# Batch normalisation on one core: tiles of even and odd channels, first tile split at a quarter

## The chip, the cores and the metric

The kernel runs on one core of one Trainium2 chip. The metric is the device time of one execution in microseconds (us). The input is read from the chip's external memory (DRAM) into the on-chip memory of 128 partitions, changed there, and written back; transfers are made by the core's 16 DMA engines. SyncE (SP) and ScalarE (ACT) each issue transfers on a queue of their own; VectorE (DVE) does most of the arithmetic.

## The reference

The input x has the shape 32 x 256 x 128 x 128 (images, channels, height, width) in float32, 537 MB. Each channel has four parameters. The whole computation is one multiplication and one addition for each element:

```python
return gamma * (x - mean) / np.sqrt(var + eps) + beta
```

With scale = gamma / sqrt(var + eps) and shift = beta - mean * scale it is out = x * scale + shift, with one scale and one shift for each channel.

## The kernel before

One image's 256 channels are two tiles of 128 channels: the lower half (channels 0 to 127) and the upper half (128 to 255). A partition holds one channel, 16384 values or 64 KB. So there are NT = 64 tiles of 8.39 MB, and a tile is one contiguous block of DRAM. Tile i uses column i % NCB (NCB is 2) of the scales and shifts.

There are three buffers for tiles (NBUF = 3), and the order of the work is written out by hand with semaphores. Each tile is loaded by SP, changed in place by VectorE (L122, one instruction with a scale and a shift for each partition), and stored by ScalarE's queue (L133). The load of tile i waits for the store of tile i - 3, which used the same buffer (L94 and the wait behind it). VectorE waits for the tile's load; the store waits for VectorE. Each queue takes its work in the order written.

Tile 0 is different: it is loaded in two parts, left (L84) and right (L91), the two halves of its columns, and VectorE changes them in two instructions. Its store waits for both. Between the two loads SP issues the four loads of parameters (L87): each brings 256 values to 16 partitions of the tile rows, which VectorE has set to zero before (L85). The last tile is different too: VectorE changes its first 9216 columns (VCOLS) and ScalarE the others (L145), side by side.

The parameters arrive with the channels along a row, and are needed with one channel in each partition. VectorE transposes rows in blocks of 32 x 32 (L100), and four copies put the blocks' first columns into the tile par (L105). ScalarE takes the square root (L107), and VectorE the reciprocal, the scale and the shift (L114 to L117). Every VectorE step here waits for the one before through the semaphore vec; the transpose waits for the four loads (the semaphore fetched) instead. The first tile's instructions follow these steps in VectorE's queue.

Of the kernel before, what the change touches and what calls it, by code (L numbers as in the profile page):

```python
# [1 line left out]

# [4 lines left out]


NBUF = 3

VCOLS = 9216


@with_exitstack
def kernel(
    ctx: ExitStack,
    tc: tile.TileContext,
    x: bass.AP,
    gamma: bass.AP,
    beta: bass.AP,  # L20
    running_mean: bass.AP,
    running_var: bass.AP,
    out: bass.AP,
):
    nc = tc.nc
    eps = 1e-5
    f32 = mybir.dt.float32

    N, C, H, W = x.shape
    P = nc.NUM_PARTITIONS  # L30
    assert C % P == 0
    NCB = C // P
    HW = H * W
    NT = N * NCB
    B = 32
    NQ = P // B
    NE = 16
    NPAR = 4

    xr = x.rearrange("n (cb p) h w -> (n cb) p (h w)", p=P)  # L40
    outr = out.rearrange("n (cb p) h w -> (n cb) p (h w)", p=P)

    params = ctx.enter_context(tc.tile_pool(name="params", bufs=1))
    data = ctx.enter_context(tc.tile_pool(name="data", bufs=1))
    bufs = [data.tile([P, HW], f32, name=f"t{s}", tag=f"t{s}") for s in range(NBUF)]
    rows = params.tile([B, NPAR * C], f32, name="rows", tag="rows")
    turned = params.tile([B, NPAR * C], f32, name="turned", tag="turned")
    par = params.tile([P, NPAR, NCB], f32, name="par", tag="par")
    eps_t = params.tile([P, 1], f32, name="eps_t", tag="eps")
    std_t = params.tile([P, NCB], f32, name="std_t", tag="std")  # L50
    rstd_t = params.tile([P, NCB], f32, name="rstd_t", tag="rstd")
    scale_t = params.tile([P, NCB], f32, name="scale_t", tag="scale")
    ms_t = params.tile([P, NCB], f32, name="ms_t", tag="ms")
    shift_t = params.tile([P, NCB], f32, name="shift_t", tag="shift")

    loaded = [tc.alloc_semaphore(f"loaded{s}") for s in range(NBUF)]
    stored = [tc.alloc_semaphore(f"stored{s}") for s in range(NBUF)]
    early = tc.alloc_semaphore("early")  # L60
    done = tc.alloc_semaphore("done")
    fetched = tc.alloc_semaphore("fetched")
    vec = tc.alloc_semaphore("vec")
    act = tc.alloc_semaphore("act")

    with tc.tile_critical():  # L66
        count = [0]

        def step(inst, sem=None, value=None):

            if sem is not None:
                inst._wait_ge(sem, value)
            elif count[0]:
                inst._wait_ge(vec, count[0])
            inst.then_inc(vec, 1)
            count[0] += 1
            return count[0]

        left, right = slice(0, HW // 2), slice(HW // 2, HW)
        last = NT - 1  # L80

        nc.sync.dma_start(out=bufs[0][:, left], in_=xr[0][:, left]).then_inc(early, 16)  # L84
        zeroed = step(nc.vector.memset(rows[:], 0.0))  # L85
        for r, ap in enumerate((running_var, gamma, beta, running_mean)):
            inst = nc.sync.dma_start(out=rows[0:NE, r * C : (r + 1) * C], in_=ap.partition_broadcast(NE))  # L87
            if r == 0:
                inst._wait_ge(vec, zeroed)
            inst.then_inc(fetched, 16)  # L90
        nc.sync.dma_start(out=bufs[0][:, right], in_=xr[0][:, right]).then_inc(loaded[0], 16)  # L91
        for i in range(1, NT):
            s, turn = i % NBUF, i // NBUF
            inst = nc.sync.dma_start(out=bufs[s][:], in_=xr[i]).then_inc(loaded[s], 16)  # L94
            if turn:
                inst._wait_ge(stored[s], 16 * turn)


        step(nc.vector.memset(eps_t[:], eps))  # L99
        step(nc.vector.transpose(out=turned[:], in_=rows[:]), fetched, 16 * NPAR)  # L100

        blocks = turned.rearrange("p (rc q b) -> p rc q b", q=NQ, b=B)
        flat = par.rearrange("p r cb -> p (r cb)")
        for q in range(NQ):
            placed = step(nc.vector.tensor_copy(out=flat[q * B : (q + 1) * B], in_=blocks[:, :, q, 0]))  # L105
        var_t, gamma_t, beta_t, mean_t = (par[:, r] for r in range(NPAR))
        nc.scalar.activation(  # L107
            out=std_t[:],
            in_=var_t,
            func=mybir.ActivationFunctionType.Sqrt,  # L110
            bias=eps_t[:],
            scale=1.0,
        )._wait_ge(vec, placed).then_inc(act, 1)
        step(nc.vector.reciprocal(out=rstd_t[:], in_=std_t[:]), act, 1)  # L114
        step(nc.vector.tensor_mul(out=scale_t[:], in0=gamma_t, in1=rstd_t[:]))  # L115
        step(nc.vector.tensor_mul(out=ms_t[:], in0=mean_t, in1=scale_t[:]))  # L116
        ready = step(nc.vector.tensor_sub(out=shift_t[:], in0=beta_t, in1=ms_t[:]))  # L117
        nc.vector.wait_ge(vec, ready)

        def compute(i, cols=slice(0, HW)):  # L120
            t, cb = bufs[i % NBUF], i % NCB
            return nc.vector.tensor_scalar(  # L122
                out=t[:, cols],
                in0=t[:, cols],
                scalar1=scale_t[:, cb : cb + 1],
                scalar2=shift_t[:, cb : cb + 1],
                op0=mybir.AluOpType.mult,
                op1=mybir.AluOpType.add,
            ).then_inc(done, 1)

        def store(i, after):
            s = i % NBUF
            nc.scalar.dma_start(out=outr[i], in_=bufs[s][:])._wait_ge(done, after).then_inc(stored[s], 16)  # L133

        compute(0, left)._wait_ge(early, 16)
        compute(0, right)._wait_ge(loaded[0], 16)
        store(0, 2)
        for i in range(1, last):
            compute(i)._wait_ge(loaded[i % NBUF], 16 * (i // NBUF + 1))
            store(i, i + 2)  # L140

        turns = last // NBUF + 1
        compute(last, slice(0, VCOLS))._wait_ge(loaded[last % NBUF], 16 * turns)
        t, cb = bufs[last % NBUF], last % NCB
        nc.scalar.activation(  # L145
            out=t[:, VCOLS:],
            in_=t[:, VCOLS:],
            func=mybir.ActivationFunctionType.Identity,
            bias=shift_t[:, cb : cb + 1],
            scale=scale_t[:, cb : cb + 1],  # L150
        )._wait_ge(loaded[last % NBUF], 16 * turns).then_inc(done, 1)
        store(last, last + 3)

        for s in range(NBUF):
            nc.sync.wait_ge(stored[s], 16 * ((NT - s + NBUF - 1) // NBUF))


# [1 line left out]
_INS = ['x', 'gamma', 'beta', 'running_mean', 'running_var']  # L159
_OUTS = [((32, 256, 128, 128), 'float32')]  # L160


# [23 lines left out]
```

## Time and profile before

| | |
|---|---|
| median of 4 runs | 2517.73 us |
| lowest and highest of them | 2506.21 and 2518.33 us |
| profiled execution, its own time | 2513.88 us |
| profiled execution, its span | 2512.1 us |
| VectorE busy | 564.0 us (22%) |
| ScalarE busy | 7.9 us |
| moved by the DMA engines | 1073.84 MB, mean 427 GB/s |
| one tile's VectorE instruction | 8.81 us |
| median from issue to landing, load and store | 63.3 and 45.3 us |
| first store issued | 28.1 us |
| last load landed, last store issued | 2483.2 and 2489.6 us |

The span is the time from the first to the last recorded instruction of the program; the execution's own time is 1.8 us longer. The row of DMA digits in a profile cuts the span in 40 slices and gives the mean busy share of the 16 DMA engines in tenths, with 9 for 90% or more. In a list of waits, a line gives who waited, for what, the sum in us, how often, and the longest. In a timeline a line gives the start and the duration in us, the engine, the line of the kernel, the operation with its output and inputs, and in brackets how long the engine sat idle before it and what ended that.

### The profile page before, as it was taken

To read this page: it belongs to the slowest core of one execution; us is meant where nothing else is said; L and a number is where in the kernel's file an instruction comes from. 1 tells how busy PE (TensorE), PEld (TensorE's weight loads), DVE (VectorE), ACT (ScalarE), POOL (GpSimd) and SP (SyncE) were. 2 spreads that over 40 slices of the span, in tenths; PEclk is the share of its full clock that TensorE was granted. 3 is DMA by queue.
4 is the path that set the end of the run, shared out by engine and by line. 5 is a ranking of instruction groups with operands and counts; after the bars stand their busy time and mean duration, and the time that the engine had idled before them with its cause. 6 is when DMAs were issued, how large, how long until landed. Compare 5 with 4: busy or idle time off the path is not lost.

```text
span 2512.1 us, 266 instructions
## 1 busy us (share of the span) xinstructions
DVE 564.0 (22%) x76; ACT 7.9 (0%) x3; POOL 0.2 (0%) x4
## 2 busy tenths in 40 slices
DVE  3121221212212122121221212212122122221221
ACT  0000000000000000000000000000000000000001
POOL 0000000000000000000000000000000000000000
DMA  9999999999999999999999999999999999999997
GB/s 418 433 432 434 433 434 433 433 433 434 429 434 431 432 433 430 431 432 429 432 422 433 420 424 431 432 433 429 422 434 431 426 430 432 423 428 428 429 431 332
DMA packets 18707, 1073.84 MB, mean 427 GB/s; under 512 B 2128, under 2 KB 2192, under 8 KB 2192
## 3 DMA queue, kind: packets, MB, share of 16 engines
q1 hardware_dynamic: 9488, 536.94, 49.9%
q10 hardware_dynamic: 9216, 536.88, 49.7%
q14 instruction: 3, 0.02, 0.0%
HBM read 536.94 MB, written 536.87 MB: 427 GB/s over the span
## 4 chain that ended last, share of the span: by engine, by line
another core or an unknown queue 76%; DVE 22%; DMA 1%; ACT 0%; issue 0%; SPq 0%; ACTq 0%; DVEq 0%
DVE t L122 22%; DMA t<-in_x_dram 1%; ACT t L145 0%; SPq L87 0%; DVE rows L85 0%; ACTq L133 0%; DVE eps_t L99 0%; DVEq L181 0%; SPq L66 0%
## 5 line engine op out<-in xcount | busy, mean ns | idle before, releaser
L122 DVE TENSOR_SCALAR t<-t,scale_t,shift_t 128x16384 f32<-128x16384 f32 (+2 forms) x65 | 560.6, 8624 | 1910.4 <-DMA t<-in_x_dram 1910.3
L145 ACT ACTIVATE t<-t,shift_t,scale_t 128x7168 f32<-128x7168 f32 x1 | 6.4, 6361 | 2466.7 <-DMA t<-in_x_dram 2466.7
L100 DVE STREAM_TRANSPOSE turned<-rows 32x1024 f32<-32x1024 f32 x1 | 1.2, 1232 | 11.9 <-DMA rows<-in_running_mean_dram 11.9
L107 ACT ACT_TABLE_LOAD x1 | 1.3, 1283 | 0.9 <-SPq L66 0.9
L85 DVE MEMSET rows<- 32x1024 f32 x1 | 0.9, 912 | 1.2 <-SPq L66 1.2
L105 DVE COPY par<-turned 32x8 f32<-32x8 f32 x4 | 0.6, 161 | 0.1
L107 ACT ACTIVATE std_t<-par,eps_t 128x2 f32<-128x2 f32 x1 | 0.3, 295 | 14.0 <-DVE par L105 14.0
L114 DVE RECIPROCAL rstd_t<-std_t 128x2 f32<-128x2 f32 x1 | 0.2, 166 | 0.4 <-ACT std_t L107 0.4
L116 DVE TENSOR_TENSOR ms_t<-par,scale_t 128x2 f32<-128x2 f32 x1 | 0.2, 161 | 0.0
L117 DVE TENSOR_TENSOR shift_t<-par,ms_t 128x2 f32<-128x2 f32 x1 | 0.2, 161 | 0.0
L115 DVE TENSOR_TENSOR scale_t<-par,rstd_t 128x2 f32<-128x2 f32 x1 | 0.2, 160 | 0.0
L170 POOL MEMSET const-bfloat16-1.0<- 128x1 bf16 x1 | 0.1, 102 | 0.0
L170 POOL MEMSET const-uint8-127<- 128x1 uint8 x1 | 0.1, 101 | 0.0
L170 POOL MEMSET const-float32-0.0<- 128x1 f32 x1 | 0.1, 99 | 0.2 <-issue 0.2
L170 POOL MEMSET const-float32-1.0<- 128x1 f32 x1 | 0.1, 98 | 0.0
L99 DVE MEMSET eps_t<- 128x1 f32 x1 | 0.1, 59 | 0.1
## 6 DMA issues: line engine op xcount, KB each, us to landing
t<-in_x_dram SPq DMA_DIRECT2D x2, 4096.0 KB, 16.1
out_dram<-t ACTq DMA_DIRECT2D x64, 45.3
t<-in_x_dram SPq DMA_DIRECT2D x63, 63.3
rows<-in_running_var_dram SPq DMA_DIRECT2D x1, 16.0 KB, 11.2
rows<-in_gamma_dram SPq DMA_DIRECT2D x1, 16.0 KB, 11.1
rows<-in_beta_dram SPq DMA_DIRECT2D x1, 16.0 KB, 10.9
rows<-in_running_mean_dram SPq DMA_DIRECT2D x1, 16.0 KB, 10.7
```

The costliest lines, as they stand in the source:

```text
L85: zeroed = step(nc.vector.memset(rows[:], 0.0))
L99: step(nc.vector.memset(eps_t[:], eps))
L100: step(nc.vector.transpose(out=turned[:], in_=rows[:]), fetched, 16 * NPAR)
L105: placed = step(nc.vector.tensor_copy(out=flat[q * B : (q + 1) * B], in_=blocks[:, :, q, 0]))
L107: nc.scalar.activation(out=std_t[:], in_=var_t, func=mybir.ActivationFunctionType.Sqrt, bias=eps_t[:], scale=1.0,)._wait_ge(vec, placed).t ...
L114: step(nc.vector.reciprocal(out=rstd_t[:], in_=std_t[:]), act, 1)
L115: step(nc.vector.tensor_mul(out=scale_t[:], in0=gamma_t, in1=rstd_t[:]))
L116: step(nc.vector.tensor_mul(out=ms_t[:], in0=mean_t, in1=scale_t[:]))
L117: ready = step(nc.vector.tensor_sub(out=shift_t[:], in0=beta_t, in1=ms_t[:]))
L122: return nc.vector.tensor_scalar(out=t[:, cols], in0=t[:, cols], scalar1=scale_t[:, cb : cb + 1], scalar2=shift_t[:, cb : cb + 1], op0=myb ...
L145: nc.scalar.activation(out=t[:, VCOLS:], in_=t[:, VCOLS:], func=mybir.ActivationFunctionType.Identity, bias=shift_t[:, cb : cb + 1], scale ...
L170: nc = _bacc.Bacc("TRN2", target_bir_lowering=False, num_devices=1)
```

## The change

A tile now holds every second channel of an image: tile 2n holds the even channels of image n, tile 2n + 1 the odd ones. Partition p holds channel 2p + cb instead of channel cb * 128 + p. In DRAM a tile's 64 KB rows then lie 128 KB apart, and the two tiles of an image share its 16.8 MB.

The parameters have to follow. A new tile lined takes a copy of rows in which the channels of each parameter are put in the new order (first the even, then the odd ones); the transpose then reads lined. The copy takes over the wait for the four loads, and the transpose waits for the copy.

The first tile is split at a quarter of its columns (4096 and 12288) instead of at half.

```diff
-    xr = x.rearrange("n (cb p) h w -> (n cb) p (h w)", p=P)
-    outr = out.rearrange("n (cb p) h w -> (n cb) p (h w)", p=P)
+
+    xv = x.rearrange("n (p cb) h w -> n cb p (h w)", cb=NCB)
+    outv = out.rearrange("n (p cb) h w -> n cb p (h w)", cb=NCB)
+    xr = [xv[i // NCB, i % NCB] for i in range(NT)]
+    outr = [outv[i // NCB, i % NCB] for i in range(NT)]
...
+    lined = params.tile([B, NPAR * C], f32, name="lined", tag="lined")
...
-        left, right = slice(0, HW // 2), slice(HW // 2, HW)
+        left, right = slice(0, HW // 4), slice(HW // 4, HW)
...
-        step(nc.vector.memset(eps_t[:], eps))
-        step(nc.vector.transpose(out=turned[:], in_=rows[:]), fetched, 16 * NPAR)
+        step(nc.vector.memset(eps_t[:], eps))
+        step(
+            nc.vector.tensor_copy(
+                out=lined.rearrange("b (r cb p) -> b r cb p", r=NPAR, cb=NCB),
+                in_=rows.rearrange("b (r p cb) -> b r cb p", r=NPAR, cb=NCB),
+            ),
+            fetched,
+            16 * NPAR,
+        )
+
+        step(nc.vector.transpose(out=turned[:], in_=lined[:]))
```

## The prediction

> **What bounds the kernel now.** I first read the page for what is busy, then the engines' waits, then the time order at both ends, and last the DMA share in stretches of one tile each.
>
> The page's busy shares, its DMA row and its issues come first:
>
> ```profile
> span 2512.1 us, 266 instructions
> DVE 564.0 (22%) x76; ACT 7.9 (0%) x3; POOL 0.2 (0%) x4
> DMA  9999999999999999999999999999999999999997
> DMA packets 18707, 1073.84 MB, mean 427 GB/s; under 512 B 2128, under 2 KB 2192, under 8 KB 2192
> q10 hardware_dynamic: 9216, 536.88, 49.7%
> t<-in_x_dram SPq DMA_DIRECT2D x63, 63.3
> ```
>
> The compute engines are idle for most of the time and the DMA engines never are, except in the last slice. The store queue's 9216 packets over 64 stores are 144 for each store. The 2128 packets under 512 B are 16 for each of the program's 133 transfers (64 stores, 69 loads). That leaves 128 data packets for one store, which is one for each partition: a packet is one channel's 64 KB row.
>
> The waits say that VectorE waits for loads and nothing else of weight, and that the load queue waits for stores:
>
> ```profile
> DVE t L122 <- DMA t<-in_x_dram: 1910.3, 64, 31.4
> SPq L94 <- DMA out_dram<-t: 2393.8, 61, 66.9
> ```
>
> One buffer's turn is closed: load 63.3 us, compute 8.8 us and store 45.3 us (medians from the page and from the instructions of L122) make 117.4 us, three times 39.1 us. So the step of a tile is 39 us, and in it 16.78 MB move (8.39 MB in, 8.39 MB out).
>
> The timeline of VectorE gives the step tile by tile, as the distance between starts. Lines 1 and 2 below are a fast step, 38.62 us; lines 3 and 4 the slowest, 40.22 us; lines 5 and 6 the fastest, 38.45 us.
>
> ```profile
> 55.46 8.81 DVE L122 TENSOR_SCALAR t<-t,scale_t,shift_t 128x16384 f32<-128x16384 f32 x1 [27.36 <-DMA t<-in_x_dram]
> 94.08 8.81 DVE L122 TENSOR_SCALAR t<-t,scale_t,shift_t 128x16384 f32<-128x16384 f32 x1 [29.80 <-DMA t<-in_x_dram]
> ...
> 1387.71 8.81 DVE L122 TENSOR_SCALAR t<-t,scale_t,shift_t 128x16384 f32<-128x16384 f32 x1 [30.63 <-DMA t<-in_x_dram]
> 1427.93 8.81 DVE L122 TENSOR_SCALAR t<-t,scale_t,shift_t 128x16384 f32<-128x16384 f32 x1 [31.41 <-DMA t<-in_x_dram]
> ...
> 2014.27 8.81 DVE L122 TENSOR_SCALAR t<-t,scale_t,shift_t 128x16384 f32<-128x16384 f32 x1 [30.04 <-DMA t<-in_x_dram]
> 2052.72 8.81 DVE L122 TENSOR_SCALAR t<-t,scale_t,shift_t 128x16384 f32<-128x16384 f32 x1 [29.64 <-DMA t<-in_x_dram]
> ```
>
> From tile 1 at 55.46 us to tile 63 at 2483.20 us there are 62 steps, 39.16 us each on average. In the stretches (columns: window, length, busy time and count of VectorE, ScalarE and GpSimd, clock, DMA share, GB/s) slow and fast tiles alike have the DMA engines full:
>
> ```profile
> 94.62:133.78 39.16, 9.33 (x2) 0.00 (x0) 0.00 (x0) 1.00 0.99 428
> 1386.90:1426.06 39.16, 8.81 (x1) 0.00 (x0) 0.00 (x0) 1.00 1.00 418
> 2170.10:2209.26 39.16, 8.81 (x1) 0.00 (x0) 0.00 (x0) 1.00 0.99 415
> ```
>
> So a slow step is not an idle one: its packets take longer. The difference of 415 to 428 GB/s at one and the same share is what the memory's side does to the packets, and it is the only thing in the trace that the address pattern could move.
>
> **The change, part by part.**
>
> *Split of tile 0 at a quarter.* The first transfer of the tile falls from 4.19 MB to 2.10 MB, the second grows from 4.19 MB to 6.29 MB; the instruction count stays. The four parameter loads are issued on SP between the two, so they sit behind 2.10 MB less: at 413 GB/s (the stretch from 10 to 20 us) they land 5.1 us earlier, the last at 9.1 us in place of 14.2. The second part ends when the whole tile has come, at 23.5 us as now. VectorE's share of it grows from 8192 to 12288 columns. By the 4.55 us of the half that is 6.8 us, by three quarters of 8.81 it is 6.6 us; I take 6.6. Store 0 is thus issued at 30.2 us in place of 28.1, which is 2.1 us late. The store of tile 0 waits in ScalarE's queue; behind it stand only later stores, which wait for later tiles anyway. Load 3 waits on SP for store 0, with all the later loads behind it. What hides it: loads 1 and 2, 16.8 MB, are queued from 4.4 us on, and the engines' share is 1.04 from 50 to 60 us. Were this cover gone, the price would be the 2.1 us themselves. The bounds are -1.0 us (the loads have the engines to themselves for 2.1 us more, half of which they gain) and +2.1 us. I take +2.1, because the buffer's turn is closed (the SP queue waited for a store 61 times out of 61), so a late store can pass its delay on.
>
> *The copy rows to lined and the wait that moves to it.* One VectorE instruction more, 32x1024 with elements two apart on the reading side. No row shows it; the nearest are the 1.23 us transpose of the same tile and the 0.91 us memset. Below, at the large TENSOR_SCALAR's rate (8.81 us for 16384 columns), it would be 0.55 us, above twice the transpose, 2.5 us. I take 1.2 us. The wait for the four loads goes from the transpose to the copy; queued behind it are the transpose and the rest of the parameter work, as before. From the start of the transpose to the first tile instruction is now 17.41 - 14.17 = 3.2 us. The first tile instruction comes at 9.1 + 1.2 + 3.2 = 13.5 us, takes 2.3 us (4096 columns) and ends at 15.8, 7.7 us before the rest of tile 0. So the copy costs nothing: the wait for that rest hides it. With the cover gone it would cost its 1.2 us.
>
> *The memset of eps_t* is issued in the same place as before and takes 0.06 us: nothing.
>
> *Even and odd channels.* A tile's rows in x and out lie 128 KB apart instead of 64 KB, over 16 MB instead of 8 MB. Loads and stores stay 64 each of 128 rows of 64 KB; the first tile's rows are cut at 16 KB instead of 32 KB. Packet count and size stay, and so does SP's and ScalarE's issue work (0.33 us each). What may change is the time of a packet. No row has this pitch, so I bound it by the steps: if all 62 were like the slowest, 62 x (40.22 - 39.16) = +66 us; if all were like the 38.62 us step, 62 x (38.62 - 39.16) = -33 us (the single 38.45 us step would make -44, but it follows slow ones and will hold some of their bytes). I take zero, the value nearest to the row: 428 GB/s in most stretches, with reads and writes to different places side by side and dips that come and go without a change of pitch.
>
> One rule speaks against this part. The Trainium skill (DMA: Bandwidth & Descriptors, Latency and other measured facts) reports copies of 16 KiB rows at 207 GB/s per direction with a row pitch of 512 KiB, falling to 103 at 4 MiB, against 214 at full rate, and advises contiguous tiles; the kernel before has them, the changed one does not. No run here shows its pitches. Taken at the 512 KiB figure the sum would be 3.4% longer, an estimate of +85 us; 128 KiB lies well short of that pitch, so by the page some part of it, by the row nothing.
>
> *The end.* The last load lands at 2483.2 us, the split of that tile between VectorE and ScalarE stays (6.36 us), and the last store follows: nothing moves but the addresses.
>
> **The sum.** +2.1 us for the first store, 0 for the copy, 0 for the pitch: +2.1 us. The profiled execution took 2513.88 us by its own time, 1.8 us more than its span of 2512.1; so it would become 2516.0. The median of the four runs is 2517.73, 3.85 us above the profiled one; on that scale the forecast is 2519.8 us. The four runs range over 12 us (2506.21 to 2518.33), so a change under 0.5%, 12.6 us, can hardly be told from none in this kernel.
>
> **The rivals.**
>
> *Slower: the wider pitch makes packets longer.* Place: the 62 steps, in the engines' packets, with the share still at 1.0. For it speak the stretches at 415 and 418 GB/s with full share; against it the 428 GB/s that most stretches hold. It decides from 0.2 us a step (12.6 / 62). Halfway to the slowest step is +0.53 us: 62 x 0.53 = +33, so 2517.7 + 33 = 2551 us. At its bound of 40.22 us a step it is 2584.
>
> *Faster: the wider pitch spares the slow steps.* Load and store of neighbouring tiles then run within the same 16 MB, one on even and one on odd rows. For it: slow steps exist at full share, so there is something to spare. Against it: at most 33 us are there. It counts from -0.2 us a step; two thirds of the bound, -22 us, give 2496 us, the whole bound 2485.
>
> *The change does nothing at the start.* If the late first store is made up by the loads, -1 us and 2517 us; if the copy, at 2.5 us, were not hidden as well, +4.6 us and 2522. Both stay within the forecast's own case.
>
> **How the numbers follow.** No mechanism of the start reaches 0.5%, so the question is the pitch alone. Within 0.5% gets 0.42: rate and share say that the engines' own pace, not the addresses, sets most steps. Slower gets 0.37, because its bound reaches twice as far as the other and a step has to grow by only 0.2 us. Faster gets 0.21: it has to remove over a third of the 33 us that are there. The likeliest case's own range is 2506 to 2530. For 8 times in 10 I go into both others: down to 2494, which leaves out the last 0.08 of the faster case, and up to 2564, near halfway between the slower rival's 2551 and its bound, which leaves out 0.12.
>
> **What would show it.** Right: the same 128 data packets a transfer, steps of 39.0 to 39.3 us, about 428 GB/s in the stretches, the copy at about 9 us with a duration near 1.2 us, the first tile instruction near 13.5 us, and the first store's issue at 30.2 us. The slower rival shows as steps over 39.4 us with the share still at 1.0 and GB/s under 425; the faster one as steps under 38.9 us. The forecast is wrong if the step's mean moves by over 0.2 us, if the share falls under 0.97 in the middle (a gap between transfers that I don't foresee), or if the first store comes later than the loads of tiles 1 and 2 can cover.

## The result: no difference that can be measured

The changed kernel takes 2510.68 us (median of 38 runs, 2489.64 to 2521.74), the kernel before 2512.64 us (median of 62 runs, 2483.82 to 2524.97). The ratio of the times is 1.0002 with a 95% interval of 0.9988 to 1.0015; the two medians, 0.1% apart, lie inside it. The profiled execution of the changed kernel took 2505.8 us, with a span of 2504.0 us. It is 8.1 us shorter than the one of before, but one execution of this kernel can differ from the next by far more than that, so the difference of the two profiles is not the change's.

The page of the changed kernel, its rows on busy shares, DMA and loads:

```profile
span 2504.0 us, 267 instructions
DVE 564.7 (23%) x77; ACT 7.9 (0%) x3; POOL 0.2 (0%) x4
DMA  9999999999999999999999999999999999999997
DMA packets 18707, 1073.84 MB, mean 429 GB/s; under 512 B 2128, under 2 KB 2192, under 8 KB 2192
q10 hardware_dynamic: 9216, 536.88, 49.5%
t<-in_x_dram SPq DMA_DIRECT2D x63, 58.1
```

The packets are as many as before, 18707 in all and 9216 on the store queue, and the row of DMA digits is the same. The one new instruction is the copy. The waits of VectorE and of the load queue are those of before to within 9 us in 1902 or 2391:

```profile
DVE t L134 <- DMA t<-in_x_dram: 1902.0, 64, 31.4
SPq L98 <- DMA out_dram<-t: 2391.1, 61, 67.4
```

The start is where the two kernels differ by construction. The first lines are of the kernel before, those in the second fence of the changed one (start, duration, engine, line; a line with x4 stands for four issues of stores, and its start is that of the first):

```profile
14.17 1.23 DVE L100 STREAM_TRANSPOSE turned<-rows 32x1024 f32<-32x1024 f32 x1 [11.92 <-DMA rows<-in_running_mean_dram]
17.41 4.55 DVE L122 TENSOR_SCALAR t<-t,scale_t,shift_t 128x8192 f32<-128x8192 f32 x1
28.13 113.77 ACTq L133 DMA_DIRECT2D out_dram<-t  x4
```

```profile
9.45 0.68 DVE L104 COPY lined<-rows 32x1024 f32<-32x1024 f32 x1 [7.20 <-DMA rows<-in_running_mean_dram]
13.41 2.41 DVE L134 TENSOR_SCALAR t<-t,scale_t,shift_t 128x4096 f32<-128x4096 f32 x1
23.46 6.68 DVE L134 TENSOR_SCALAR t<-t,scale_t,shift_t 128x12288 f32<-128x12288 f32 x1 [7.64 <-DMA t<-in_x_dram]
30.17 110.22 ACTq L145 DMA_DIRECT2D out_dram<-t  x4
53.46 8.81 DVE L134 TENSOR_SCALAR t<-t,scale_t,shift_t 128x16384 f32<-128x16384 f32 x1 [23.32 <-DMA t<-in_x_dram]
```

The parameters come in at 9.45 us instead of 14.17, and the first tile instruction starts at 13.41 instead of 17.41. All of that ends in an idle time of 7.64 us, since the rest of tile 0 lands at 23.46 us. The first store is issued 2.0 us later than before (30.17 against 28.13), and tile 1 starts 2.0 us earlier (53.46 against 55.46).

From tile 1 to tile 63 (2470.94 us) the changed kernel needs 62 steps of 38.99 us on average, before 39.16. Three stretches of one step each, an ordinary, the slowest and one of the fastest (window, length, busy time of VectorE, ScalarE and GpSimd, clock, DMA share, GB/s):

```profile
92.28:131.21 38.93, 8.81 (x2) 0.00 (x0) 0.00 (x0) 1.00 1.00 431
367.50:407.76 40.26, 8.81 (x2) 0.00 (x0) 0.00 (x0) 1.00 0.98 420
1696.52:1735.16 38.64, 8.81 (x2) 0.00 (x0) 0.00 (x0) 1.00 1.01 436
```

The slowest and the fast step are like those of before (40.22 and 38.62 us there). Slow steps still exist, at a full share, with the wider pitch.

### The profile page after: what moved, and what is told of

It is laid out like the page before. It is cut to its first block, busy times and chain, and to the rows that moved or that the text cites. A ratio compares the mean times of both kernels' runs of the same rounds, so it can differ in the third digit from the quotient of the medians.

```text
span 2504.0 us, 267 instructions
## 1 busy us (share of the span) xinstructions
DVE 564.7 (23%) x77; ACT 7.9 (0%) x3; POOL 0.2 (0%) x4
## 2 busy tenths in 40 slices
DMA packets 18707, 1073.84 MB, mean 429 GB/s; under 512 B 2128, under 2 KB 2192, under 8 KB 2192
## 3 DMA queue, kind: packets, MB, share of 16 engines
q10 hardware_dynamic: 9216, 536.88, 49.5%
## 4 chain that ended last, share of the span: by engine, by line
another core or an unknown queue 75%; DVE 22%; DMA 2%; ACT 0%; issue 0%; SPq 0%; ACTq 0%; DVEq 0%
DVE t L134 22%; DMA t<-in_x_dram 2%; ACT t L157 0%; SPq L91 0%; DVE rows L89 0%; SPq L95 0%; ACTq L145 0%; DVE eps_t L102 0%; DVEq L193 0%; SPq L70 0%
```

## The experiments

Two theories were to be told apart at first: that the DMA engines' own pace sets the step, whatever the rows' pitch of 64 or 128 KB; and that the two parts of the change each do something and cancel.

**Each part alone.** The first kernel is the changed one with the old split, the second the old one with the new split.

```diff
# even and odd channels alone
-        left, right = slice(0, HW // 4), slice(HW // 4, HW)
+        left, right = slice(0, HW // 2), slice(HW // 2, HW)
# split alone, from the kernel before
-        left, right = slice(0, HW // 2), slice(HW // 2, HW)
+        left, right = slice(0, HW // 4), slice(HW // 4, HW)
```

> Even and odd channels with the copy, the first tile still split at half. Theory 'the engines' own pace sets the step': ratio to before 0.997 to 1.003, steps near 39.1 us, parameters landed at 14.2 us and the first store near 29 us (the copy's 0.68 us in front of the first tile's first half may now show, since that half waits only for the parameters). Rival 'the wide pitch costs and the new split gives it back': ratio over 1.005 here and under 0.995 for the split alone; the other way round if the pitch gains and the split costs.

> Tiles contiguous as before, no copy, the first tile split at a quarter. Theory 'engines' pace': ratio 0.997 to 1.003, first store issued at 30.2 us against 28.1, tile 1 starting 1 to 2 us earlier (53.5 to 54.5 us), because its load has the engines to itself for longer. Rival 'the two parts cancel': ratio outside 0.995 to 1.005. Rival 'a late first store is passed on to the end': +2.1 us, which is too little to be told from none by the ratio, but the mean step and the end would be those of before, shifted.

Even and odd channels alone: ratio 1.0031 (0.9973 to 1.0090). The split alone: 0.9988 (0.9929 to 1.0046). Neither differs from 1, where the theory of cancelling needed more than 0.5% in both, with opposite signs. The intervals leave room for opposite parts of up to 0.7%, but nothing in the runs asks for them. With the old split the copy does stand in front of the first half, which starts at 18.01 us instead of 17.41; but it still ends before the other half lands (23.33 us), so the first store is issued at 27.91 us and the copy is hidden here too. With the split alone the first store is issued at 30.33 us and tile 1 starts at 52.98, so the shifts at the start come from the split.

The profile of the split alone is of an execution of 2484.52 us. Its page:

```profile
span 2482.7 us, 266 instructions
DMA  9999999999999999999999999999999999999999
GB/s 417 429 438 435 428 435 439 430 432 438 435 429 437 439 427 435 439 431 431 438 436 429 435 437 428 433 439 432 431 438 437 429 435 439 428 434 434 428 438 400
```

It moves 433 GB/s in the mean and has no idle slice at the end. That is not the split's doing: the kernel before took from 2483.41 us to over 2520 us on that chip, with the same code and the same pitch.

**How far the pitch can grow.** If 128 KB does nothing, a larger pitch shows whether the address pattern matters at all. These kernels read and write the tensor as rows of 64 KB, K rows apart:

```diff
-    xr = x.rearrange("n (cb p) h w -> (n cb) p (h w)", p=P)
-    outr = out.rearrange("n (cb p) h w -> (n cb) p (h w)", p=P)
+    K = 8
+    xf = x.rearrange("n c h w -> (n c) (h w)").rearrange("(a p k) f -> a k p f", p=P, k=K)
+    outf = out.rearrange("n c h w -> (n c) (h w)").rearrange("(a p k) f -> a k p f", p=P, k=K)
+    xr = [xf[i // K, i % K] for i in range(NT)]
+    outr = [outf[i // K, i % K] for i in range(NT)]
```

K is 8, 16, 32 or 64, for 512 KB, 1 MB, 2 MB and 4 MB.

> Rows 512 KB apart (every eighth row of 1024), four times the pitch of the change, loads and stores alike; each row gets the scale and the shift of another channel, so only the time is read. Theory 'engines' pace, the pitch is no matter in this range': ratio 0.995 to 1.005, DMA at 425 to 430 GB/s. Rival 'the pitch costs, and 128 KB was only too little to see it': steps of 39.4 to 40.5 us, ratio 1.01 to 1.035. The Trainium skill (DMA: Bandwidth & Descriptors, Latency and other measured facts) has 207 GB/s against 214 for rows 512 KiB apart, which would be a ratio of 1.03.

> Rows 4 MB apart: each of the 64 tiles takes every 64th row of the whole tensor; each row gets the scale and the shift of another channel, so only the time is read. If the pitch never matters the ratio is within 0.995 to 1.005. If there is a pitch from which it matters, this one should show it: steps well over 40 us with the DMA share still near 1.0 and packets longer, ratio anywhere from 1.05 up. The Trainium skill (same page and section) has 103 GB/s against 214 at 4 MiB, which would be a ratio of 2.0.

> Rows 1 MB apart for loads and stores; each row gets another channel's scale and shift, so only the time is read. Known: 512 KB gave 1.0054 (0.9986 to 1.0122), 4 MB gave 1.348. If the cost grows steadily with the pitch, this lies at 1.01 to 1.05; if there is an edge beyond it, at 0.998 to 1.01.

> The same with rows 2 MB apart. Steady growth: 1.08 to 1.20, halfway to the 4 MB case. An edge between 2 and 4 MB: under 1.02. The Trainium skill (DMA: Bandwidth & Descriptors, Latency and other measured facts) has 164 GB/s against 214 at 2 MiB, which would be a ratio of 1.30.

| Pitch of the rows | Ratio to before | 95% interval |
|---|---|---|
| 128 KB (even and odd channels alone) | 1.0031 | 0.9973 to 1.0090 |
| 512 KB | 1.0054 | 0.9986 to 1.0122 |
| 1 MB | 1.0268 | 1.0185 to 1.0351 |
| 2 MB | 1.0540 | 1.0461 to 1.0619 |
| 4 MB | 1.3479 | 1.3370 to 1.3588 |

So the pitch does matter, and from 1 MB on it can be measured; 128 KB is well below that. The theory that it never matters falls, the theory that it costs something already at 128 KB is not supported. At 512 KB the ratio lies between the two expectations, and its interval reaches from nothing to 1.2%. Between 2 and 4 MB the cost grows sixfold, so it is neither a straight line nor a clean edge. All these pitches are powers of two; whether the distance costs or the power of two was not tried. The figures of the Trainium skill (DMA: Bandwidth & Descriptors, Latency and other measured facts), measured with 16 KiB rows, have the right sign and are too large for these 64 KB rows: as an estimate from them, the ratios would be 1.03 at 512 KiB, 1.30 at 2 MiB and 2.08 at 4 MiB.

The traces hold every packet with its start and its duration, and these show what sets the step. In the profiled execution of the kernel before, 95% of the 16256 packets of 64 KB took 2.40 to 2.44 us, most of them 2.418 us, and none took less; in that of the changed kernel it is 96%. Sixteen engines at 2.418 us a packet move 434 GB/s, an estimate from these numbers that is close to the 433 GB/s of the split alone. A few packets take longer: in the kernel before 12% of those that started in its slowest step took over 2.5 us, 1% in its step from 55.46 us. With the pitch the share at the common pace falls, to 91% at 512 KB and 86% at 1 MB; with the split alone, at the narrow pitch, it is 98%, each from one execution. So the wide pitch costs by making some packets longer, and at 128 KB nothing of this is seen.

The page of the 1 MB case shows where its cost falls in the execution:

```profile
span 2548.3 us, 266 instructions
DMA  9999999999999999999999999999999999999998
GB/s 361 398 409 406 428 430 423 425 426 424 425 422 432 427 431 427 429 428 427 430 426 426 429 428 429 432 424 432 422 427 426 426 431 428 430 431 428 434 426 314
```

The first four slices of 64 us move 361 to 409 GB/s, the others mostly 422 to 434, although every tile has the same pitch. The first 16 packets start within 1.4 us of each other. That the 16 engines get out of each other's way later, and that this is why the cost fades, fits the row but was not tried; at 4 MB on one side it does not fade away, as the stretches from the middle of two executions below show.

**Which side pays.** The 4 MB pitch on one side only:

```diff
# loads alone: stores as before
-    outr = [outf[i // K, i % K] for i in range(NT)]
+    outr = out.rearrange("n (cb p) h w -> (n cb) p (h w)", p=P)
# stores alone: loads as before
-    xr = [xf[i // K, i % K] for i in range(NT)]
+    xr = x.rearrange("n (cb p) h w -> (n cb) p (h w)", p=P)
```

> Loads with rows 4 MB apart, stores contiguous; rows of out are written from other rows of x, so only the time is read. If the cost is on the reads' side, most of the 0.348 of both comes back here (1.25 to 1.35) and the stores alone give little; if each side has its own half, 1.12 to 1.22 in both; if it takes both sides at once, both stay under 1.05.

> Stores with rows 4 MB apart, loads contiguous; rows of out are written from other rows of x, so only the time is read. Writes' side: 1.25 to 1.35; each side its half: 1.12 to 1.22; reads' side or both needed: under 1.05.

Loads alone: 1.0834 (1.0767 to 1.0902). Stores alone: 1.1716 (1.1621 to 1.1811). The stores cost twice as much as the loads, and the two add up to 0.255, short of the 0.348 that they cost together. None of the three patterns named beforehand fits: both sides pay by themselves, unequally, and more when they come together. The middle of the two executions, that of the wide loads first:

```profile
1000.00:1200.00 200.00, 44.06 (x5) 0.00 (x0) 0.00 (x0) 1.00 1.00 406
```

```profile
1000.00:1200.00 200.00, 41.48 (x5) 0.00 (x0) 0.00 (x0) 1.00 1.00 373
```

The packets differ by side. With the loads 4 MB apart, 44% of the load packets took over 2.5 us and 3% of the store packets, as against 5% and 3% in the kernel before. With the stores 4 MB apart it is 61% of the load packets, though the loads are contiguous, and 46% of the store packets. So wide stores make the packets of both sides longer and wide loads only their own, which is where the stores' higher price lies.

The DMA share is 1.00 in both, as in the kernel before, where such stretches move 427 to 432 GB/s. This is what a cost of the address pattern looks like: full engines and fewer bytes. A share of 1.00 alone does not say that the engines run at their best.

**Is a late first store passed on?** The prediction took the 2.1 us of the late first store into its sum. Two kernels make that store much later, with memsets of a spare tile between the two parts of tile 0:

```diff
         compute(0, left)._wait_ge(early, 16)
+        for _ in range(21):
+            step(nc.vector.memset(spare[:], 0.0))
         compute(0, right)._wait_ge(loaded[0], 16)
```

> Before, with 21 memsets of 32x1024 (0.91 us each, about 20 us) on VectorE between the two parts of tile 0, so that store 0 is issued at about 46 us in place of 28.1. Theory 'loads 1 and 2 cover a late first store': the DMA engines stay full (they have loads until about 62 us), the ratio is 0.997 to 1.003. Rival 'the buffer's turn is closed, a late store is passed on': +18 us, ratio 1.007.

> The same with 64 memsets (about 60 us): store 0 at about 86 us. Both theories have a loss here. Cover: loads 1 and 2 end at about 62 us, the engines are idle for the 24 us from then to the store, and the time grows by about 24 us, ratio 1.008 to 1.011. Passed on: +58 us, ratio 1.023.

With 21 memsets the first store was issued at 51.09 us, 23 us late. The ratio is 0.9975 (0.9935 to 1.0015): nothing that could be measured is passed on, at most 4 us by the interval, where 23 us would be 1.009. The first store, and stretches of 10 us in this kernel while it is late (a packet counts in the stretch in which it starts, so a share can come out over 1):

```profile
51.09 122.77 ACTq L134 DMA_DIRECT2D out_dram<-t  x5
...
30.00:40.00 10.00, 7.60 (x10) 0.00 (x0) 0.00 (x0) 1.00 1.09 472
40.00:50.00 10.00, 8.66 (x7) 0.00 (x0) 0.00 (x0) 1.00 0.97 419
50.00:60.00 10.00, 9.77 (x2) 0.00 (x0) 0.00 (x0) 1.00 1.01 419
60.00:70.00 10.00, 0.26 (x1) 0.00 (x0) 0.00 (x0) 1.00 0.97 419
```

Loads fill the engines until the store comes. With 64 memsets they can't (the last line is the first store):

```profile
50.00:60.00 10.00, 7.60 (x10) 0.00 (x0) 0.00 (x0) 1.00 0.97 419
60.00:70.00 10.00, 7.86 (x9) 0.00 (x0) 0.00 (x0) 1.00 0.00 1
...
90.00:100.00 10.00, 8.40 (x8) 0.00 (x0) 0.00 (x0) 1.00 0.00 0
...
101.55 76.68 ACTq L134 DMA_DIRECT2D out_dram<-t  x4
```

The last packets of the three tiles that there are buffers for start before 60 us and end at 62 us, and from then until the first store, issued at 101.55 us, nothing moves. The store is 73 us late. It came later than expected, as each memset took 1.18 us with the wait for the one before, not 0.94. The ratio of 1.0187 (1.0132 to 1.0242) is 33 to 60 us of the 2497.31 us that the kernel before took on that chip, 47 in the middle. The idle time of about 40 us lies in this range; the 73 us of the delay (a ratio of 1.029) do not. So a late store costs the part that the loads can't cover, and up to some 34 us of delay (from 28.1 us to the 62 us at which the loads' packets end) that should be nothing; of this, 23 us were tried.

**The idle time at the end.** At the end of the kernel before the DMA engines are partly idle (shares of 0.70 and 0.23 in the two lines below, 10.7 us in sum), and in the changed kernel as well, in the second fence (0.47 and 0.46):

```profile
2470.00:2480.00 10.00, 0.00 (x0) 0.00 (x0) 0.00 (x0) 1.00 0.70 301
2480.00:2490.00 10.00, 5.08 (x1) 6.36 (x1) 0.00 (x0) 1.00 0.23 98
```

```profile
2460.00:2470.00 10.00, 0.00 (x0) 0.00 (x0) 0.00 (x0) 1.00 0.47 203
2470.00:2480.00 10.00, 5.08 (x1) 6.36 (x1) 0.00 (x0) 1.00 0.46 197
```

This is the one place where the profile shows time that could be had, so a kernel from the one before cuts the last tile into four parts, each loaded, changed and stored by itself.

```diff
+        parts = [slice(a * HW // 8, z * HW // 8) for a, z in ((0, 4), (4, 6), (6, 7), (7, 8))]
+        for k, cols in enumerate(parts):
+            inst = nc.sync.dma_start(out=bufs[s][:, cols], in_=xr[last][:, cols]).then_inc(tails[k], 16)
...
+        for k, cols in enumerate(parts):
+            compute(last, cols)._wait_ge(tails[k], 16)
+            inst = nc.scalar.dma_start(out=outr[last][:, cols], in_=bufs[last % NBUF][:, cols])
+            inst._wait_ge(done, last + 2 + k).then_inc(shut, 16)
```

> Before, with the last tile cut in four parts of its columns (8192, 4096, 2048, 2048), each loaded, changed by VectorE and stored by itself, ScalarE's share gone. In the profile of before the DMA engines stood idle for 10.7 us in sum between 2470 and 2490 us (shares 0.70 and 0.23). If that idle time is the wait for the whole tile and its arithmetic, the last stores start earlier and 5 to 8 us go, ratio 0.997 to 0.998; if it is engines that ran ahead of others and had nothing left to do, it stays and the ratio is 0.999 to 1.001.

The ratio is 1.0005 (0.9959 to 1.0051): nothing found, though an interval of this width can't exclude the expected 0.25%. Some of its stretches at the end, of 5 us:

```profile
2474.00:2479.00 5.00, 3.55 (x1) 0.00 (x0) 0.00 (x0) 1.00 0.52 226
...
2489.00:2494.00 5.00, 1.63 (x1) 0.00 (x0) 0.00 (x0) 1.00 0.30 129
...
2499.00:2504.00 5.00, 1.34 (x1) 0.00 (x0) 0.00 (x0) 1.00 0.42 177
```

In this execution the idle time is spread over the parts instead of gone. The packets' starts and durations show why. In the kernel before 16 packets are in progress at any time until 2474 us, and just 6 from 2476 to 2484 us, while the last tile is still landing; in the changed kernel it is 4 to 6 from 2465 to 2477 us, where its last tile lands at 2470.94, and in the kernel with four parts 5 from 2489.5 to 2494 us. So the engines come to the end at different times: some still have work and the others have none. Which engines these are, and why they are late, stays open. No version was found that beats both kernels.

## Why the prediction was right, and where it was not

The forecast was no measurable change, and that is what came; the case had a chance of 0.42.

- *The pitch, taken at zero.* Right for 128 KB: 1.0031 with an interval that includes 1, and steps as fast and as slow as before. The mean step of 38.99 us lies just under the 39.0 to 39.3 us that were named, in one profile. The reason given, that the engines' pace and not the addresses sets most steps, is borne out at 128 KB by the packets, 96% of them at one and the same pace; from 1 MB on it fails. That a slow step holds longer packets is borne out for the slowest step of before. That the memory's side makes them longer at the narrow pitch was argued, and no run shows it.
- *The rival of slower packets* described a real mechanism, with the very sign it was to show (share at 1.0, GB/s below 425), but it can be measured only at eight times the pitch of the change. Its price was worked out from slow steps that have nothing to do with the pitch: they are as slow, 40.26 us, with the wide one.
- *The rival of faster packets* falls: the slow steps of before are not spared.
- *The first store* was issued at 30.17 us where 30.2 was forecast, but the step from there to the end failed. The closed turn of a buffer was taken as a reason to count the 2.1 us as lost; a store 23 us late cost nothing that could be measured. The bound of the sum should have been read from what is queued on the DMA engines, as the prediction did when it named the cover, and not from the number of waits. Without this term the forecast on its own scale is 2517.7 us.
- *The loads' gain* was put at 1.0 us, for half of the engines during 2.1 us; tile 1 starts 2.0 us earlier. Why it is the whole of it was not settled, and it does not reach the end.
- *The copy* was taken at 1.2 us and took 0.68, near its lower bound of 0.55; it is hidden, as forecast, with 7.64 us of idle time behind it. The first tile instruction came at 13.41 us, forecast 13.5; this is so close by luck, since the parameters came 0.35 us later than forecast (9.45 for 9.1) and the copy took 0.52 us less.
- *The scale.* The forecast went up from a profiled execution to a median of four runs, 2517.73 us. With 62 runs the median of before is 2512.64. Of the 9.1 us between the forecast and 2510.68 us, 5.1 are this and 2.1 the term for the first store; the other 2 us are too few to be told from none.

## What to carry to other kernels

When transfers bound a kernel, ask of a change at its edges whether the DMA engines still have queued work: here a first store could be 23 us late at no measurable cost, and one 73 us late cost about what lay beyond the cover. Full DMA engines say that nothing waits for compute, not that the bytes move at best speed; read the share and the GB/s together. Interleaving rows of 64 KB at 128 KB cost nothing that could be measured here, but rows 1 MB apart and more did, and at 4 MB, the one pitch tried on each side alone, the stores cost more than the loads.

## What was not expected of the hardware

- A 4 MB pitch costs 17.2% on the stores alone and 8.3% on the loads alone, and 34.8% on both, more than the sum.
- The 1 MB pitch costs most in the first 255 us (361 to 409 GB/s) and little later (mostly 422 to 434).
- One and the same program, the kernel before, took between about 2483 and 2525 us in its 62 executions, with the granted clock at 1.0 throughout. The one profiled execution near the lower end, of the split alone, moves 433 GB/s in the mean, and 1.2% of its 64 KB packets took over 2.5 us, against 4.3% in the profile of the kernel before.
- Wide stores lengthen the packets of contiguous loads as well (61% over 2.5 us, against 5% before); wide loads leave the packets of contiguous stores as they are (3%).
